# Three elementwise steps of an RWKV layer, from GpSimd to VectorE

## The chip, the cores and the metric

The kernel runs on one core of one Trainium2 chip. The metric is the device time of one execution in microseconds (us); the time of a kernel is the median of its runs.

## The reference, cut to what matters

A two-layer decoder over 1024 tokens of width 1024. The first layer is latent attention, the second an RWKV-7 mixer with 24 heads of width 64; each has four memory heads beside it, a SiLU gate and an output projection. All that the change touches is in the second layer:

```python
w = -jax.nn.softplus(-(w0 + jnp.tanh(wd) @ w2)) - 0.5
decay = jnp.exp(-jnp.exp(w))
a = jax.nn.sigmoid(a0 + ad @ a2)
kk = heads(k * k_k)
kk = kk / jnp.maximum(jnp.linalg.norm(kk, axis=-1, keepdims=True), 1e-12)
k = k * (1.0 + (a - 1.0) * k_a)
# one step of the scan
sa = jnp.einsum('bhvk,bhk->bhv', state, -kk_t)
state = state * w_t[:, :, None, :] + sa[..., None] * (kk_t * a_t)[:, :, None, :] + v_t[..., None] * k_t[:, :, None, :]
# after the scan
y = (y - mean) * lax.rsqrt(var + GN_EPS)
y = y * gn_w + gn_b
```

## The kernel before, in words

Activations lie with channels on the 128 partitions and 512 tokens along the free axis, so each of the two halves of the sequence is a tile of 128x512. A large matmul is done as three: every fp32 operand is split into a high part (rounded, fp32r) and a low part (the rest), and high by high, high by low and low by high are summed (mm3, L159 to L164). ScalarE (ACT) makes the high part of a weight tile (L153), and VectorE (DVE) or GpSimd (POOL) the low part (L155). In the RWKV layer VectorE makes all the low parts of the large weights.

The RWKV layer works through 24 items: 12 pairs of heads for the first half of the tokens, then the same 12 for the second half. An item passes five stages, and five items are under way at a time, one in each stage (layer1, the loop over `stages`):

- `project`: r, k and v by large matmuls;
- `prep`: the small decay weights w2 and a2 are loaded and split (L990 to L992) and multiplied (L996, L997); k is normed to kk (L1003 to L1016, with the reciprocal root of `rsqrt`, L194 to L199); then k is scaled (L1019), a is multiplied by kk (L1020), r*k is formed for the bonus (L1024), summed over a head by a matmul with a block of ones (L1042), and kk, r, a and k are scaled by the decay (L1049 to L1058);
- `invert`: 31 pairs of small VectorE instructions (L1139, L1143) solve triangular systems;
- `scan`: eight chunks one after the other, each a chain TensorE (L1215, L1217), VectorE (gm, L1219), TensorE (L1221), VectorE (SAV, L1222), TensorE (L1224), VectorE (the new state S, L1236);
- `norm`: squares, sum and `rsqrt` of the outputs (tile m), the scaling of the outputs by it (L1265), transposes on TensorE (L1269) and two VectorE steps (L1270, L1271).

The gate and output projections, large matmuls in groups of three (L162 to L164), are interleaved with these. A scheduler writes the final order of each engine's queue when the program is built, and each engine then works through its queue in that order; an instruction at the head of a queue that waits for another engine holds up all that stands behind it. The three tiles of the small weights (w2, w2h, w2l) have one buffer each, so the next item's split waits until this item's matmuls L996 and L997 have read them.

Of the kernel before, what the change touches and what calls it, by code (L numbers as in the profile page):

```python
# [13 lines left out]
F32 = mybir.dt.float32  # L14
# [4 lines left out]
ALU = mybir.AluOpType  # L19
# [52 lines left out]
class Build:  # L72
# [706 lines left out]
    def layer1(self, x1, first, second):  # L779

        nc, A, tc = self.nc, self.A, self.tc
        with ExitStack() as st:
# [158 lines left out]
            self.lows = True  # L941
            N, now = 2 * NH, [0]
            stages = [(project, ST[0]), (lambda i: self.prep(items[i], env), ST[1]), (lambda i: self.invert(items[i], env), ST[2]), (scan, ST[3]), (norm, ST[4])]
            extra = {}
            add = lambda step, gen, n: extra.setdefault(step, []).append((gen, n + 1))
# [33 lines left out]
    def prep(self, d, env):  # L979
# [6 lines left out]
        V, G, ACT = nc.vector, nc.gpsimd, nc.scalar  # L986
        ck = lambda t: t[:].rearrange("p (c t) -> p c t", t=64)

        w2, wh, wl = (self.w2p.tile([P, 256], dt, tag=s, name=self.name(s)) for s, dt in (("w2", F32), ("w2h", F32R), ("w2l", F32R)))
        nc.sync.dma_start(w2[:], self.A["w2a2"][p])  # L990
        ACT.copy(wh[:], w2[:])  # L991
        G.tensor_sub(wl[:], w2[:], wh[:].bitcast(F32))  # L992
        sig, a = self.g(s="sig"), self.g(s="a")
        for j, (t, bias) in enumerate(((sig, PW0), (a, PA0))):
            ps = a_tile()
# [19 lines left out]
        kk = sq  # L1015
# [1 line left out]
        rk = self.g(s="rk")  # L1017
        ACT.activation(rk[:], a[:], AF.Identity, bias=self.oka[:, p : p + 1], scale=self.pc(PKA + p))
        V.tensor_mul(k[:], rk[:], k[:])  # L1019
        G.tensor_mul(a[:], a[:], kk[:])  # L1020

        yield

# [59 lines left out]
        for i in range(4):  # L1083
            yield
            ps = a_tile()
            for j in range(2):
# [4 lines left out]
                out=AM[i][:], in0=ps[:].rearrange("p (c f) -> p c f", f=256),  # L1091
                in1=am.unsqueeze(1).broadcast_to([P, 2, 256]), op=ALU.mult,
# [158 lines left out]
    def norm(self, d, env):  # L1251

        p, bonus, Y, sg, y_tile = d["p"], d["bonus"], d["Y"], d["sg"], env["y_tile"]
        nc = self.nc
        V, G, ACT = nc.vector, nc.gpsimd, nc.scalar
        yg = Y[:].rearrange("p i (h v) -> p (i h) v", h=2)
        m = self.smp.tile([P, 24], F32, tag="m", bufs=2, name=self.name("m"))
        wide = lambda x: x.unsqueeze(2).broadcast_to([P, 8, 64])
        ys = self.g([P, 8, 64], s="ys")
        ACT.activation(ys[:], yg, AF.Square)  # L1260
        V.tensor_reduce(m[:, 8:16], ys[:], AX.X, ALU.add)
        V.tensor_scalar(m[:, 8:16], m[:, 8:16], 1.0 / 64, EPS_G, ALU.mult, ALU.add)
        self.rsqrt(m, 8)
        yield
        G.tensor_tensor(out=yg, in0=yg, in1=wide(m[:, 0:8]), op=ALU.mult)  # L1265
        yield
        ps = y_tile()
        for i in range(4):
            nc.tensor.transpose(ps[:, i * P : i * P + P], Y[:, i, :], self.ident)  # L1269
        V.scalar_tensor_tensor(bonus[:], ps[:], self.pc(PGW + p), bonus[:], ALU.mult, ALU.add)  # L1270
        V.scalar_tensor_tensor(sg[:], bonus[:], self.pc(PGB + p), sg[:], ALU.add, ALU.mult)  # L1271
# [107 lines left out]
```

## Time and profile before

| | before |
|---|---|
| median of 3 runs | 2585.66 us (2582.15 to 2588.03) |
| the profiled execution: its time, its span | 2576.96 us, 2575.1 us |
| granted TensorE clock over the span | 0.991 |
| the RWKV layer's items, from the first product a * kk to the end | about 1040 us to 2575 us |
| GpSimd: L1020, L1265, L992 | 24 instructions each |

A row of groups names the source line, engine, operation, output and inputs (buffer numbers left out), the shape and the count, then the time busy and the mean duration in ns, then the idle time of the engine just before, with what ended it. A row of the timeline begins with the start and the duration in us. A row of waits says which engine waited for what: us in total, how often, the longest. PE is TensorE's matmuls and PEld its weight loads; the ends of matmuls are modelled.

### The profile page before, as it was taken

The numbers are of one execution on the slowest core, as the hardware profiler recorded it, in microseconds if no ns is written. First come the engines' busy times: TensorE is split into PE (matmuls) and PEld (weight loads), VectorE is DVE, ScalarE is ACT, GpSimd is POOL, SyncE is SP. The second block draws the span as 40 slices with busy tenths as digits, with TensorE's granted clock in tenths as the row PEclk, the third lists the DMA queues.
The fourth block names the chain that finished last, engine by engine and source line by source line (L and its number), as shares of the span: only waits on it lengthen the run. The fifth ranks groups of instructions, "written<-read, shape, count | busy, mean of one in ns | idle before, by whom it ended". The sixth has DMA issues, their size and how long they took to land.

```text
span 2575.1 us, 39906 instructions
## 1 busy us (share of the span) xinstructions
PE 2440.8 (95%) x13298; PEld 2004.1 (78%) x13298; DVE 1897.9 (74%) x5492; ACT 1374.2 (53%) x2971; POOL 367.7 (14%) x416
## 2 busy tenths in 40 slices
PE   7899999999999999999999999999999999999997
PEld 5687778888888788877777777777777777778775
DVE  6755334777777646698888888788888888786975
ACT  5444335555545434565665666666665655654542
POOL 4332222222211330010000000000000010000000
PEclk9999999999999999999999999999999999999998
DMA  4252222111112444422122222322222222232341
GB/s 161 86 172 89 80 82 76 47 59 50 56 60 70 142 158 145 139 79 74 61 65 74 77 74 83 103 78 78 70 77 73 69 85 94 94 99 96 107 146 68
DMA packets 165983, 231.46 MB, mean 90 GB/s; under 512 B 46096, under 2 KB 67984, under 8 KB 165776
## 3 DMA queue, kind: packets, MB, share of 16 engines
q1 hardware_dynamic: 165776, 228.90, 27.1%
q8 instruction: 105, 1.72, 0.3%
q14 instruction: 102, 0.84, 0.1%
HBM read 187.66 MB, written 37.49 MB: 87 GB/s over the span
## 4 chain that ended last, share of the span: by engine, by line
PE 64%; DVE 19%; ACT 5%; issue 5%; DMA 2%; SPq 0%; POOL 0%; POOLq 0%; DVEq 0%; ACTq 0%
PE mm L162 12%; PE mm L164 12%; PE mm L163 12%; PE a L1088 3%; DVE U L1143 2%; DVE tmp L1139 2%; PE pt L726 2%; DVE wl L155 2%; PE po L162 1%; PE po L163 1%; PE c L1221 1%; PE po L164 1%; PE c L1224 1%; DVE u L1019 1%; PE c L1215 1%
## 5 line engine op out<-in xcount | busy, mean ns | idle before, releaser
L153 ACT CAST wh<-wr 128x512 fp32r<-128x512 f32 (+3 forms) x500 | 298.7, 600 | 442.8 <-PE mm L163 362.8
L162 PE MATMUL mm<-xnh,wh 128*128 128x512 f32 x912 | 376.5, 413 | 0.6 <-DVE qml L134 0.4
L164 PE MATMUL mm<-xnh,wl 128*128 128x512 f32 x912 | 370.7, 407 | 1.1 <-DVE wl L155 1.1
L163 PE MATMUL mm<-xnl,wh 128*128 128x512 f32 x912 | 370.0, 406 | 0.0
L155 DVE TENSOR_TENSOR wl<-wr,wh 128x512 fp32r<-128x512 f32 (+2 forms) x352 | 238.5, 679 | 115.8 <-ACT wh L153 84.2
L155 POOL TENSOR_TENSOR wl<-wr,wh 128x512 fp32r<-128x512 f32 (+1 forms) x148 | 186.5, 1264 | 575.9 <-ACT wh L153 445.0
L162 PE MATMUL mm<-yh,wh 128*128 128x512 f32 x492 | 199.7, 406 | 5.9 <-DVE xr L391 5.9
L164 PE MATMUL mm<-yh,wl 128*128 128x512 f32 x492 | 196.3, 399 | 0.2 <-DVE wl L155 0.2
L162 PEld LDWEIGHTS mm<-xnh,wh 128*128 128x128 f32 x912 | 172.7, 190 | 30.4 <-issue 3.3
L164 PEld LDWEIGHTS mm<-xnh,wl 128*128 128x128 f32 x912 | 172.6, 189 | 29.9 <-DVE wl L155 1.3
L163 PE MATMUL mm<-yl,wh 128*128 128x512 f32 x492 | 195.4, 397 | 0.0
L163 PEld LDWEIGHTS mm<-xnl,wh 128*128 128x128 f32 x912 | 173.0, 190 | 26.1 <-issue 0.8
L162 PE MATMUL mm<-xh,wh 128*128 128x512 f32 x416 | 168.1, 405 | 7.7 <-ACT xh L440 7.7
L1235 ACT ACTIVATE sc<-S,f 128x128 f32<-128x128 f32 x168 | 67.4, 401 | 195.3 <-DVE S L1236 184.0
L1143 DVE TENSOR_TENSOR U<-U,tmp 128x60 f32<-128x60 f32 (+24 forms) x744 | 159.7, 215 | 13.5
L163 PE MATMUL mm<-xl,wh 128*128 128x512 f32 x416 | 167.5, 403 | 2.0 <-DVE xl L441 2.0
L164 PE MATMUL mm<-xh,wl 128*128 128x512 f32 x416 | 167.1, 402 | 0.0
L1139 DVE TENSOR_TENSOR tmp<-As,U 128x60 f32<-128x60 f32 (+24 forms) x744 | 157.1, 211 | 13.3 <-DMA U<-in_cst_dram 0.2
L992 POOL TENSOR_TENSOR w2l<-w,w2h 128x256 fp32r<-128x256 f32 x24 | 20.8, 865 | 897.9 <-ACT w2h L991 859.4
L304 ACT ACTIVATE p<-b,sm 128x512 f32<-128x512 f32 (+2 forms) x144 | 83.0, 580 | 117.5 <-DVE sm L301 78.2
L391 DVE TENSOR_TENSOR xr<-mm,xr 128x512 f32<-128x512 f32 x123 | 84.4, 688 | 77.2 <-PE mm L164 76.8
L162 PEld LDWEIGHTS mm<-yh,wh 128*128 128x128 f32 x492 | 92.8, 189 | 24.3 <-DVE xr L391 3.8
(362 smaller groups left out, 6300.0 us busy)
## 6 DMA issues: line engine op xcount, KB each, us to landing
wr<-in_wu_dram SPq DMA_DIRECT2D x292, 256.0 KB, 2.6
wr<-in_wo_dram SPq DMA_DIRECT2D x122, 256.0 KB, 2.6
yr<-y SPq DMA_DIRECT2D x60, 256.0 KB, 3.7
As<-sysd SPq DMA_DIRECT2D x24, 512.0 KB, 4.3
y<-y SPq DMA_DIRECT2D x32, 256.0 KB, 2.0
y<-sg SPq DMA_DIRECT2D x32, 256.0 KB, 2.1
g<-u SPq DMA_DIRECT2D x24, 256.0 KB, 2.5
gt<-g SPq DMA_DIRECT2D x24, 256.0 KB, 2.8
```

Source lines behind the costliest of these rows:

```text
L153: nc.scalar.copy(hi[:, :n], raw[:, :n])
L155: sub(lo[:, :n], raw[:, :n], hi[:, :n].bitcast(F32))
L162: mm(ps, a[0], b[0], start=start, stop=False)
L163: mm(ps, a[0], b[1], start=False, stop=False)
L164: mm(ps, a[1], b[0], start=False, stop=stop)
L304: nc.scalar.activation(p[:, :own], ps[:, :own], AF.Exp, bias=sm[:, 0:1], accum_out=sm[:, 2 + i : 3 + i])
L391: nc.vector.tensor_add(xs[m][:], ps[:], xs[m][:])
L726: nc.tensor.transpose(pt[:, o : o + P], src, self.ident)
L1088: mm(ps[:, j * 256 : j * 256 + 256], BK[c // 4][:, c % 4, :], AR[:, c, :], start=True, stop=True)
L1139: E.tensor_tensor(out=tmp[:, 0:u, 0:n], in0=As[:, 0:u, u : u + 1].broadcast_to([P, u, n]), in1=U[:, u : u + 1, i0:8].broadcast_to([P, u, n ...
L1143: E.tensor_tensor(out=U[:, 0:u, i0:8], in0=U[:, 0:u, i0:8], in1=tmp[:, 0:u, 0:n], op=ALU.add)
L1235: ACT.activation(sc[:], cur, AF.Copy, scale=fc)
```

## The change

Three calls in `prep` and `norm` go from GpSimd to VectorE, operands and shapes as before: the low part of the small decay weights (w2l, 128x256), the product a * kk (128x512) and the scaling of the normed outputs (yT, 128x512). The memset of SAV (L1069) stays on GpSimd.

```diff
@@ prep
         ACT.copy(wh[:], w2[:])
-        G.tensor_sub(wl[:], w2[:], wh[:].bitcast(F32))
+        V.tensor_sub(wl[:], w2[:], wh[:].bitcast(F32))
@@ prep
         V.tensor_mul(k[:], rk[:], k[:])
-        G.tensor_mul(a[:], a[:], kk[:])
+        V.tensor_mul(a[:], a[:], kk[:])
@@ norm
         yield
-        G.tensor_tensor(out=yg, in0=yg, in1=wide(m[:, 0:8]), op=ALU.mult)
+        V.tensor_tensor(out=yg, in0=yg, in1=wide(m[:, 0:8]), op=ALU.mult)
```

The scheduler writes all queues anew from there on, so it is not only that 72 rows change engine. VectorE's queue in `prep` of the third item (k is u_2537, kk is sq_2580), before:

```order
L1016 SCALAR_TENSOR_TENSOR sq_2580_11877<-u_2537_11666,prm_102,a_2583_11898 128x512
L1143 TENSOR_TENSOR U_2570_11828<-U_2570_11828,tmp_2571_11829 128x20x3
L1019 TENSOR_TENSOR u_2537_11666<-rk_2584_11912,u_2537_11666 128x512
L1049 TENSOR_TENSOR sig_2565_11816<-sq_2580_11877,sig_2565_11816 128x512
L1024 SCALAR_TENSOR_TENSOR rk_2584_11912<-u_2520_11562,prm_102,u_2537_11666 128x512
L1057 TENSOR_TENSOR BK_2609_12011<-a_2566_11817,Dm_2593_11932 128x4x64
```

The same place after the change:

```order
L1016 SCALAR_TENSOR_TENSOR sq_2580_11877<-u_2537_11666,prm_102,a_2583_11898 128x512
L1139 TENSOR_TENSOR tmp_2571_11829<-As_2569_11826,U_2570_11828 128x19x4
L1019 TENSOR_TENSOR u_2537_11666<-rk_2584_11912,u_2537_11666 128x512
L1020 TENSOR_TENSOR a_2566_11817<-a_2566_11817,sq_2580_11877 128x512
L1024 SCALAR_TENSOR_TENSOR rk_2584_11912<-u_2520_11562,prm_102,u_2537_11666 128x512
L1049 TENSOR_TENSOR sig_2565_11816<-sq_2580_11877,sig_2565_11816 128x512
L1057 TENSOR_TENSOR BK_2609_12011<-a_2566_11817,Dm_2593_11932 128x4x64
```

The product a * kk (L1020) now stands ahead of L1024, whose result TensorE's L1042 reads, and L1049 has moved behind L1024. So it is with all 24 items: L1020 stands between L1019 and L1024; before, L1049 stood between them in 12 of the 24.

VectorE's queue in the scan of an item of the first half (S0_2828 is the state, gm_2916 the next chunk's first step), before:

```order
L1222 COPY SAV_2613_12040<-c_2901_13361 64x128
L1236 SCALAR_TENSOR_TENSOR S0_2828_13048<-c_2902_13364,f_2594_11936,sc_2903_13368 128x128
L155 TENSOR_TENSOR wl_2966_13665<-wr_2964_13663,wh_2965_13664 128x512
L1219 TENSOR_TENSOR gm_2916_13444<-c_2915_13441,cst_101 128x128
L829 SCALAR_TENSOR_TENSOR u_2911_13408<-mm_2910_13383,prm_102,u_2911_13408 128x511
```

The same place after the change:

```order
L829 SCALAR_TENSOR_TENSOR u_2911_13408<-mm_2910_13383,prm_102,u_2911_13408 128x511
L1139 TENSOR_TENSOR tmp_2812_12944<-As_2810_12941,U_2811_12943 128x24
L1222 COPY SAV_2613_12040<-c_2901_13361 64x128
L1143 TENSOR_TENSOR U_2811_12943<-U_2811_12943,tmp_2812_12944 128x24
L155 TENSOR_TENSOR wl_2966_13665<-wr_2964_13663,wh_2965_13664 128x512
L1139 TENSOR_TENSOR tmp_2812_12944<-As_2810_12941,U_2811_12943 128x16
L1236 SCALAR_TENSOR_TENSOR S0_2828_13048<-c_2902_13364,f_2594_11936,sc_2903_13368 128x128
L1143 TENSOR_TENSOR U_2811_12943<-U_2811_12943,tmp_2812_12944 128x16
L992 TENSOR_TENSOR w2l_3049_14067<-w2_3047_14065,w2h_3048_14066 128x256
L1139 TENSOR_TENSOR tmp_2812_12944<-As_2810_12941,U_2811_12943 128x8
L1143 TENSOR_TENSOR U_2811_12943<-U_2811_12943,tmp_2812_12944 128x8
L1219 TENSOR_TENSOR gm_2916_13444<-c_2915_13441,cst_101 128x128
```

The low part of the next item's small weights (L992) stands between one chunk's state (L1236) and the next chunk's gm (L1219), and waits there for ScalarE's w2h_3048.

VectorE's queue after the change at the last item's outputs (yT_5946), close to the end of the program:

```order
L198 SCALAR_TENSOR_TENSOR m_6058_27611<-m_6058_27611 128x8
L199 SCALAR_TENSOR_TENSOR m_6058_27611<-m_6058_27611 128x8
L1265 TENSOR_TENSOR yT_5946_27185<-yT_5946_27185,m_6058_27611 128x512
L155 TENSOR_TENSOR wl_6074_27669<-wr_6072_27667,wh_6073_27668 128x128
L155 TENSOR_TENSOR wl_6077_27678<-wr_6075_27676,wh_6076_27677 128x128
L1270 SCALAR_TENSOR_TENSOR rk_5666_25952<-y_6065_27641,prm_102,rk_5666_25952 128x512
```

Before, the same rows stood there without L1265, which was GpSimd's; the two low parts L155 now stand behind it.

## The prediction

> **What bounds the kernel now.** I read the page's busy times and chain first, then the stages of the RWKV layer, then the three GpSimd groups and what they overlap, then TensorE's waits. The page:
>
> ```profile
> PE 2440.8 (95%) x13298; PEld 2004.1 (78%) x13298; DVE 1897.9 (74%) x5492; ACT 1374.2 (53%) x2971; POOL 367.7 (14%) x416
> PE 64%; DVE 19%; ACT 5%; issue 5%; DMA 2%; SPq 0%; POOL 0%; POOLq 0%; DVEq 0%; ACTq 0%
> ```
>
> TensorE is busy 95% of the span, and the chain that ended last runs over it and, a fifth of the time, over VectorE; GpSimd's share of that chain is 0%. So a faster product or scaling on its own buys nothing. The RWKV layer in six stretches (columns: PE, PEld, DVE, ACT and POOL busy, each with its count):
>
> ```profile
> 1040.00:1250.00 210.00, 200.35 (x1047) 160.24 (x1046) 177.31 (x568) 129.15 (x269) 18.75 (x22) 1.00 0.26 85
> 1250.00:1500.00 250.00, 234.26 (x1331) 191.84 (x1330) 206.55 (x710) 145.03 (x326) 18.21 (x20) 1.00 0.24 76
> 1500.00:1750.00 250.00, 238.47 (x1297) 190.37 (x1295) 212.54 (x700) 161.58 (x349) 17.29 (x20) 1.00 0.25 81
> 1750.00:2000.00 250.00, 238.36 (x1351) 192.33 (x1351) 210.35 (x718) 157.79 (x353) 19.65 (x21) 1.00 0.24 78
> 2000.00:2250.00 250.00, 237.24 (x1307) 191.11 (x1308) 207.47 (x721) 149.55 (x325) 21.05 (x24) 0.99 0.26 84
> 2250.00:2575.00 325.00, 298.20 (x1581) 243.06 (x1579) 247.51 (x749) 146.33 (x323) 10.99 (x12) 0.98 0.30 102
> ```
>
> Over these 1535 us TensorE is busy 1446.9 and idle 88; VectorE is busy 1261.7 (82%) and idle 273. The matmuls stay as they are, so the most that the change could win is part of the 88 us, and it can lose where VectorE's fuller queue makes TensorE wait.
>
> **What VectorE gets.** The three groups that leave GpSimd:
>
> ```profile
> L1020 POOL TENSOR_TENSOR a<-a,sq 128x512 f32<-128x512 f32 x24 | 34.9, 1454 | 146.0 <-DVE sq L1016 134.5 <-DVE S L1236 6.3 <-DVE wl L155 5.1
> L1265 POOL TENSOR_TENSOR yT<-yT,m 128x512 f32<-128x512 f32 x24 | 28.7, 1196 | 407.8 <-DVE n L198 121.0 <-DVE m L199 111.3 <-DVE n L199 62.1
> L992 POOL TENSOR_TENSOR w2l<-w,w2h 128x256 fp32r<-128x256 f32 x24 | 20.8, 865 | 897.9 <-ACT w2h L991 859.4
> ```
>
> Their price on VectorE comes from neighbours of the same form, the first a plain product, the second a difference with a broadcast operand, the third the low part of a 128x256 tile:
>
> ```profile
> L1050 DVE TENSOR_TENSOR L<-u,L 128x512 f32<-128x512 f32 x24 | 16.3, 681 | 0.0
> L1029 DVE TENSOR_TENSOR Dm<-L 128x512 f32<-128x512 f32 x24 | 16.4, 682 | 0.0
> L129 DVE TENSOR_TENSOR mks<-mkr,mks 128x256 fp32r<-128x256 f32 x8 | 3.4, 422 | 0.6 <-ACT mks L128 0.3
> ```
>
> That is 24 x 0.681 + 24 x 0.682 + 24 x 0.422 = 16.3 + 16.4 + 10.1 = 42.8 us.
>
> **What VectorE loses.** The timeline shows VectorE standing still beside GpSimd's instructions. At the product:
>
> ```profile
> 1293.70 0.73 DVE L829 SCALAR_TENSOR_TENSOR u<-mm,prm,u 128x511 f32<-128x511 f32 x1
> 1294.21 1.29 POOL L1020 TENSOR_TENSOR a<-a,sq 128x512 f32<-128x512 f32 x1 [6.52 <-DVE sq L1016]
> 1294.36 1.69 DVE L1019 TENSOR_TENSOR u<-rk,u 128x512 f32<-128x512 f32 x1
> ...
> 1295.97 0.34 DVE L1236 SCALAR_TENSOR_TENSOR S<-c,f,sc 128x128 f32<-128x128 f32 x1
> ```
>
> L1019 has the form of L1050 but takes 1.69 us: it begins 0.15 us behind GpSimd's L1020 and ends 0.55 us after it, most of its own 0.68 us after GpSimd let go. And at the outputs:
>
> ```profile
> 1285.79 1.90 POOL L1265 TENSOR_TENSOR yT<-yT,m 128x512 f32<-128x512 f32 x1 [12.72 <-DVE n L197]
> ...
> 1286.77 0.94 DVE L198 SCALAR_TENSOR_TENSOR n<-n 128x8 f32<-128x8 f32 x1
> ```
>
> An instruction over 8 columns takes 0.94 us and ends with GpSimd's. The groups show that this is the rule:
>
> ```profile
> L1019 DVE TENSOR_TENSOR u<-rk,u 128x512 f32<-128x512 f32 x24 | 30.0, 1249 | 0.0
> L1049 DVE TENSOR_TENSOR sig<-sq,sig 128x512 f32<-128x512 f32 x24 | 19.6, 817 | 0.0
> L1024 DVE SCALAR_TENSOR_TENSOR rk<-u,prm,u 128x512 f32<-128x512 f32 x24 | 18.7, 781 | 0.0
> L1016 DVE SCALAR_TENSOR_TENSOR sq<-u,prm,a 128x512 f32<-128x512 f32 x24 | 17.8, 742 | 1.2 <-PE a L1013 1.1
> L198 DVE SCALAR_TENSOR_TENSOR n<-n 128x8 f32<-128x8 f32 x81 | 20.6, 255 | 0.1
> L198 DVE SCALAR_TENSOR_TENSOR m<-m 128x8 f32<-128x8 f32 x72 | 11.8, 163 | 0.2
> ```
>
> Against L1050, L1019 loses 30.0 - 16.3 = 13.7 us and L1049 3.3; against L1016, L1024 loses 0.9: 17.9 us, 51% of L1020's 34.9. The n rows of L198 lose 81 x (0.255 - 0.163) = 7.5 us, mostly beside L1265. So the floor of what VectorE gets back is 25.4 us, and the ceiling the three groups' whole 84.4 us. I take the 51% that L1020 shows for all three: 43 us. VectorE's net is then 0, between +17 and -42 us.
>
> The Trainium skill, "SBUF — State Buffer", section "Who interferes with whom", says why: a VectorE instruction with two inputs in SBUF and a GpSimd instruction that reads SBUF share a read port, and whichever starts second is blocked whole. By that rule the loss is the overlap and vanishes with the GpSimd instructions; the rows of L1019 agree (1249 ns against 681).
>
> **What lies on the path.** TensorE's longest waits in this layer, where the changed steps stand in front of it:
>
> ```profile
> PE a L1042 <- DVE rk L1024: 12.0, 15, 1.6
> PE c L1221 <- DVE gm L1219: 9.4, 17, 1.1
> PE a L1013 <- ACT sq L1010: 5.7, 7, 1.5
> PE c L1221 <- DVE m L198: 5.6, 4, 1.6
> ```
>
> *The product.* L1042 waits for L1024, which stands behind L1019. Before, the collisions put on that stretch, per item, 0.57 us (L1019) and (3.3 + 0.9) / 24 = 0.17 us (L1049, L1024), and in 12 of 24 items L1049 itself stands in it. After, L1020 stands in it always. Instructions of this size follow each other at 0.66 us (1293.70 to 1294.36 above). Per item: +0.66 - 0.57 - 0.17 - 0.66 x 12/24 = -0.41 us. Fifteen waits cut by 0.41 are 6.2 us; as some of the 15 are shorter than that, I take -5, between -10 (all but the shortest gone) and +2 (L1049, now late, is missed by ScalarE's copies behind it). What is late next is L1042's own place in TensorE's queue; the large matmuls ahead of it have room to move up.
>
> *The scaling of the outputs.* The neighbours of L1265 in VectorE's queue are the other rsqrt (n), whose end ScalarE's L1010 and then L1013 wait for, and gm. Before they lost up to 0.94 - 0.16 = 0.78 us per collision, after they stand behind 0.66. Of the 5.7 and 5.6 us above I take -1, between -11 and +3.
>
> *The small weights.* On GpSimd L992 waited 859 us for ScalarE in an otherwise empty queue, which cost nothing. On VectorE such a wait would hold the scan up. Here is one of seven places, of 24, where the new queue puts L992 (between S and gm) ahead of the moment at which w2h was ready before:
>
> ```profile
> 1267.78 0.35 DVE L1236 SCALAR_TENSOR_TENSOR S<-c,f,sc 128x128 f32<-128x128 f32 x1 [0.71 <-PE c L1224]
> ...
> 1269.04 0.29 DVE L1219 TENSOR_TENSOR gm<-c,cst 128x128 f32<-128x128 f32 x1
> ...
> 1271.81 0.41 ACT L991 CAST w2h<-w 128x256 fp32r<-128x256 f32 x1
> ...
> 1272.34 0.72 POOL L992 TENSOR_TENSOR w2l<-w,w2h 128x256 fp32r<-128x256 f32 x1 [25.66 <-ACT w2h L991]
> ```
>
> If nothing else moved, VectorE would stand from 1268.13 to 1272.22, 4.1 us. But TensorE's and ScalarE's queues are rewritten too: L996 and L997, which free the buffers, stand one chunk earlier in the new queue. I take 0; the other end is the rival below.
>
> *The end.* The last scaling, the only one for which TensorE visibly waits on GpSimd:
>
> ```profile
> 2537.91 0.17 DVE L199 SCALAR_TENSOR_TENSOR m<-m 128x8 f32<-128x8 f32 x1
> ...
> 2538.21 1.20 POOL L1265 TENSOR_TENSOR yT<-yT,m 128x512 f32<-128x512 f32 x1 [44.95 <-ACT wh L153]
> 2539.46 0.66 PE L1269 MATMUL y<-cst,yT 128*128 128x128 f32 x4 [1.56 <-POOL yT L1265]
> ```
>
> On VectorE it starts when L199 ends (2538.08) and ends 0.68 later at 2538.76 instead of 2539.41: -0.6 us. The two low parts behind it come 0.7 us later, under the same wait.
>
> **The sum.** -5 - 1 + 0 - 0.6 = -6.6 us. The profiled execution took 2576.96 us (span 2575.1), so 2570.4. It is 8.7 us below the median of the three runs, 2585.66, and 5.2 below the fastest of them; on the median the same difference gives **2579.1 us**, -0.26%.
>
> **The rivals.**
>
> *The waits go wholly.* TensorE's queue, if written as though VectorE were never held up, fits only after the change: then the 12.0 us of L1042 and the 5.6 of L1221 behind m vanish: 2585.66 - 12.0 - 5.6 - 0.6 = 2567.5. For it: these waits stand beside collisions. Against: TensorE also waits 9.4 us for gm, in 17 waits, and nothing in these rows ties those to GpSimd.
>
> *Nothing is left.* Queues that are written anew give back at other places what L1042 wins: of 88 us idle, 6.6 are soon dealt out again. 2585.7. For it: VectorE's net is 0, and the number of waits is large and each small.
>
> *VectorE stands at the head of its queue for w2h* (slower). Seven places at 4.1 us are 29 us in which gm, SAV and S cannot run. VectorE's idle time takes some back; with half of it reaching TensorE, 2579.1 + 14.5 = 2593.6. It decides from about 2 us at each of the seven (14 us, half of it 7, which eats the gain). For it: single buffers, and GpSimd's 859 us of waiting; against: L996 and L997 moved as well.
>
> *VectorE is the bound* (slower). If the long L1019 had another cause, VectorE would take on 42.8 us and give back none: its idle time falls from 273 to 230 us, by 16%; with TensorE's idle time growing alike, 88 x 0.16 = 14 us, and 0.33 us (0.66 less half of it) at 15 waits of L1042, 5 us: 2604.7. The timeline speaks against it. The Trainium skill, "Perfetto Trace Analysis", section "Optimizing Scalar/DVE Operations", says that work may be handed to GpSimd when VectorE is saturated, the opposite of this change, but adds that the shared port may void it; at 82% busy and with the collisions above, the trace sides with the second half.
>
> **How the numbers follow.** My forecast 0.42, the waits gone wholly 0.15, nothing left 0.20, the head of the queue 0.16, VectorE the bound 0.07. The rewritten order gives each a spread of some 5 us either way, an estimate (a twentieth of the 88). About 0.2%, 5.2 us, is what a measurement of this kernel can tell from no change, so the line lies at 2580.5: faster gets 0.27 of my forecast, the 0.15 and 0.03 of "nothing left", 0.45; within 0.2% gets 0.15 of the forecast, 0.14 of "nothing left" and 0.03 of the head of the queue, 0.32; slower the remaining 0.23. The range 2564 to 2598 holds the forecast, "wholly" less 3.5 us of its spread, and the head of the queue with 4.4 us of its; it leaves out VectorE as the bound and the tails.
>
> **What would show it.** Right: L1019, L1049 and L1050 all near 0.68 us; L198 (n) near 0.16; VectorE's busy time in the six stretches within 10 us of 1261.7; TensorE's wait on L1024 at 6 to 8 us instead of 12.0; L1269 at the end behind VectorE by about 0.6 us sooner. Wrong: L1019 still near 1.2 us; an idle time before VectorE's L992 of over 14 us put down to ScalarE's w2h; TensorE idle for 88 us or more in this layer.

## The result, and the profile after

| | before | after |
|---|---|---|
| median of 4 runs each, same chip | 2583.90 us (2580.30 to 2588.03) | 2543.18 us (2540.26 to 2545.34) |
| ratio, with its 95% interval | | 0.9833 (0.9810 to 0.9856) |
| the profiled execution: time, span | 2576.96 us, 2575.1 us | 2544.33 us, 2542.6 us |
| granted TensorE clock | 0.991 | 0.991 |

The change is faster by 40.7 us between the medians. The forecast was 6.6 us: the direction was right, the size six times too small, and the time lies below the range. The two profiled executions, both at a granted clock of 0.991, lie 32.6 us apart; before's is quicker than all four of its runs in the table.

Part of the 40.7 us goes with the granted clock, the share of its full speed that TensorE was granted over a run. The kernel before, timed again with each set of experiments, took 2584.22 to 2589.57 us in its runs at 0.987 and 2578.75 to 2580.78 us in those at 0.990. One straight line through the 88 runs whose clock is on record, with one slope for all kernels, gives 2.0 us for each 0.001 of clock. Brought to one clock by this line, the change is 36 us faster, an estimate that is good to about 2 us, as are all below that are said to be at one clock. Why the clock differs between kernels is not shown.

The page after, the rows for the engines and for the chain:

```profile
PE 2434.1 (96%) x13298; PEld 2003.9 (79%) x13298; DVE 1883.6 (74%) x5564; ACT 1371.9 (54%) x2971; POOL 285.0 (11%) x344
PE 69%; DVE 16%; ACT 6%; issue 3%; DMA 2%; SPq 0%; DVEq 0%; POOL 0%; ACTq 0%; POOLq 0%
```

VectorE has 72 instructions more and is busy 14 us less; its share of the chain falls from 19% to 16%, TensorE's rises from 64% to 69%. The RWKV layer in the same stretches as before (PE, PEld, DVE, ACT, POOL), and their sum:

```profile
1040.00:1250.00 210.00, 205.17 (x1076) 165.64 (x1074) 176.07 (x578) 133.34 (x279) 4.24 (x8) 1.00 0.28 91
1250.00:1500.00 250.00, 241.56 (x1372) 197.82 (x1371) 213.05 (x767) 148.80 (x341) 4.14 (x8) 1.00 0.25 79
1500.00:1750.00 250.00, 242.34 (x1334) 196.17 (x1333) 210.03 (x708) 160.57 (x339) 4.05 (x8) 1.00 0.26 84
1750.00:2000.00 250.00, 241.78 (x1369) 195.42 (x1368) 215.61 (x774) 167.33 (x373) 5.27 (x10) 1.00 0.24 76
2000.00:2250.00 250.00, 242.35 (x1367) 196.88 (x1365) 210.41 (x735) 148.37 (x332) 4.16 (x8) 1.00 0.29 91
2250.00:2543.00 293.00, 269.62 (x1417) 219.60 (x1416) 225.55 (x680) 132.00 (x287) 2.03 (x4) 0.97 0.31 104
sum 1503.00, PE 1442.82 PEld 1171.53 DVE 1250.72 ACT 890.41 POOL 23.90; mean PE 240.47 PEld 195.26 DVE 208.45 ACT 148.40 POOL 3.98
```

The layer is 32 us shorter (1535 to 1503), and 28 us of that is TensorE's idle time: 1535 - 1446.9 = 88 us before, 1503 - 1442.8 = 60 after. Every stretch has some of it: in each of the four middle ones TensorE is busy 241.6 to 242.4 of 250 us, where it was 234.3 to 238.5. VectorE's groups after:

```profile
L1265 DVE TENSOR_TENSOR yT<-yT,m 128x512 f32<-128x512 f32 x24 | 16.6, 690 | 0.1
L1020 DVE TENSOR_TENSOR a<-a,sq 128x512 f32<-128x512 f32 x24 | 16.5, 686 | 0.0
L1049 DVE TENSOR_TENSOR sig<-sq,sig 128x512 f32<-128x512 f32 x24 | 16.4, 684 | 0.0
L1019 DVE TENSOR_TENSOR u<-rk,u 128x512 f32<-128x512 f32 x24 | 16.4, 682 | 0.0
L198 DVE SCALAR_TENSOR_TENSOR n<-n 128x8 f32<-128x8 f32 x81 | 13.2, 163 | 0.1
L992 DVE TENSOR_TENSOR w2l<-w,w2h 128x256 fp32r<-128x256 f32 x23 | 9.7, 420 | 1.0 <-ACT w2h L991 1.0
```

The moved instructions cost what their neighbours cost (690, 686, 420 ns). L1019 is down from 1249 to 682 ns, L198 (n) from 255 to 163. L992 waits for w2h 1.0 us in all. TensorE's waits in the layer:

```profile
PE y L1269 <- ACT yT L1244: 4.8, 19, 0.6
...
PE a L1042 <- DVE rk L1024: 3.3, 4, 1.4
PE c L1221 <- DVE gm L1219: 3.1, 8, 1.0
PE c L1221 <- DVE m L195: 1.8, 2, 1.0
PE a L1013 <- ACT sq L1010: 0.8, 4, 0.3
```

L1042 waits 3.3 us instead of 12.0, L1221 behind gm 3.1 instead of 9.4 and behind m 1.8 instead of 5.6, L1013 0.8 instead of 5.7. Together these four rows fell by 23.7 us, most of the 28; some smaller waits grew. And the end of the program in the timeline:

```profile
2505.85 0.17 DVE L199 SCALAR_TENSOR_TENSOR m<-m 128x8 f32<-128x8 f32 x1
2506.05 0.69 DVE L1265 TENSOR_TENSOR yT<-yT,m 128x512 f32<-128x512 f32 x1
...
2506.89 0.63 PE L1269 MATMUL y<-cst,yT 128*128 128x128 f32 x4 [0.72 <-DVE yT L1265]
```

From L199's end to L1269's start it is 2506.89 - 2506.02 = 0.87 us, before 2539.46 - 2538.08 = 1.38.

### The profile page after: what moved, and what is told of

It is laid out like the page before. It is cut to its first block, busy times and chain, and to the rows that moved or that the text cites. A ratio compares the mean times of both kernels' runs of the same rounds, so it can differ in the third digit from the quotient of the medians.

```text
span 2542.6 us, 39928 instructions
## 1 busy us (share of the span) xinstructions
PE 2434.1 (96%) x13298; PEld 2003.9 (79%) x13298; DVE 1883.6 (74%) x5564; ACT 1371.9 (54%) x2971; POOL 285.0 (11%) x344
## 4 chain that ended last, share of the span: by engine, by line
PE 69%; DVE 16%; ACT 6%; issue 3%; DMA 2%; SPq 0%; DVEq 0%; POOL 0%; ACTq 0%; POOLq 0%
PE mm L162 14%; PE mm L163 13%; PE mm L164 13%; PE a L1088 3%; DVE tmp L1139 2%; PE c L1221 2%; PE pt L726 2%; DVE U L1143 2%; PE c L1224 1%; PE po L162 1%; PE y L1228 1%; PE po L163 1%; DVE wl L155 1%; PE y L1227 1%; PE po L164 1%
## 5 line engine op out<-in xcount | busy, mean ns | idle before, releaser
L155 DVE TENSOR_TENSOR wl<-wr,wh 128x512 fp32r<-128x512 f32 (+2 forms) x352 | 237.2, 676 | 98.7 <-ACT wh L153 79.8
L155 POOL TENSOR_TENSOR wl<-wr,wh 128x512 fp32r<-128x512 f32 (+1 forms) x148 | 186.3, 1263 | 579.4 <-ACT wh L153 446.0
L1069 POOL MEMSET SAV<- 64x512 f32 x48 | 24.9, 524 | 1385.6 <-DVE m L1261 250.7
```

The source lines that it names most:

```text
L155: sub(lo[:, :n], raw[:, :n], hi[:, :n].bitcast(F32))
```

## The experiments

"Standstill" below is counted in each trace instruction by instruction: what a VectorE instruction that overlaps a GpSimd one takes beyond the lower quartile of its own line and shape. Before, this gives 21.2 us beside L1020, 13.9 beside L1265 and 8.4 beside L992, 43.5 in all; after, 0. (VectorE's busy time in the layer, with the same queue, falls by 39.5 us from before to x_free, 1261.7 to 1222.2, so the count is good to some 10%.) Theory: these standstills cost time almost one to one, because the queues were written as if they did not exist. First rival: the time comes from the rewritten queues, whatever VectorE gets back. Second rival: it is a matter of how much work VectorE has. A third, the prediction's own, is the place of the product ahead of L1024. A fourth is the granted clock, which was 0.985 to 0.988 in the runs of e2_norm and 0.991 to 0.993 in those of i_rope; the last column takes it out by the line of 2.0 us for each 0.001.

| run | what it is | median, us | ratio (95%) | less than before, us | the same at one clock (estimate) |
|---|---|---|---|---|---|
| x_free | before's queues, GpSimd reads next to nothing | 2543.74 | 0.9844 (0.9827 to 0.9861) | 41.5 | 40 |
| x_collide | the change's queues, 72 spare readers on GpSimd | 2573.81 | 0.9956 (0.9939 to 0.9972) | 11.4 | 9 |
| x_known | the change, the same 72 on VectorE | 2560.99 | 0.9915 (0.9893 to 0.9936) | 24.7 | 23 |
| f_prod | before's queues, no product on GpSimd | 2569.95 | 0.9942 (0.9925 to 0.9959) | 15.8 | 14 |
| f_norm | before's queues, no scaling on GpSimd | 2572.43 | 0.9950 (0.9931 to 0.9970) | 13.3 | 13 |
| e1_prod | only the product moved | 2566.10 | 0.9935 (0.9919 to 0.9952) | 19.1 | 18 |
| e2_norm | only the scaling moved | 2582.80 | 0.9994 (0.9985 to 1.0003) | 2.4 | 5 |
| e12_prodnorm | these two moved | 2552.33 | 0.9876 (0.9860 to 0.9892) | 33.4 | 29 |
| e3_w2l | only the small weights moved | 2575.05 | 0.9969 (0.9955 to 0.9982) | 9.2 | 6 |
| i_swap | the change, product ahead of the scaling of k | 2552.30 | 0.9876 (0.9860 to 0.9892) | 32.0 | 31 |
| i_late | the change, product behind the bonus | 2548.98 | 0.9866 (0.9845 to 0.9886) | 35.3 | 33 |
| i_rope | the change, and three steps of the first layer | 2535.72 | 0.9813 (0.9796 to 0.9829) | 48.6 | 41 |

The column before the last is taken between medians that were timed together; before's lay between 2584.3 and 2585.72 us.

### Standstill or queues: x_free and x_collide

x_free keeps the queues of TensorE, VectorE and ScalarE exactly as before. What GpSimd read becomes a memset, which reads nothing, but for 8 of the product's 512 columns; the kernel leaves this work out:

```diff
-        G.tensor_sub(wl[:], w2[:], wh[:].bitcast(F32))
+        G.memset(wl[:].bitcast(F32), 0.0)
...
-        G.tensor_mul(a[:], a[:], kk[:])
+        G.tensor_mul(a[:, 0:8], a[:, 0:8], kk[:, 0:8]); G.memset(a[:, 8:T], 0.5)
...
-        G.tensor_tensor(out=yg, in0=yg, in1=wide(m[:, 0:8]), op=ALU.mult)
+        G.memset(Y[:], 0.0)
```

> The kernel before with every queue of TensorE, VectorE and ScalarE in the order of before, but GpSimd no longer reads in the three places: the low part of the small weights and the scaling of the outputs are GpSimd memsets (0), and of the product a * kk only 8 of 512 columns are formed, the others set to 0.5 (this work is left out). Theory C (collisions: the gain of 41 us came from VectorE no longer standing still beside GpSimd): nothing is added to VectorE and the standstills go, so at least the gain of the change, 2530 to 2550 us, with L1019 near 0.68 us and TensorE's idle time in the RWKV layer some 25 to 45 us lower. Theory Q (queues: the gain came from the scheduler's new order, the collisions cost little): 2572 to 2584 us.

It took 2543.74 us, as fast as the change (2543.18) by the medians and some 4 us faster at one clock, with not one row of these three queues moved. The layer as one stretch, then two of VectorE's groups and one of GpSimd's:

```profile
1040.00:2542.00 1502.00, 1443.45 (x7910) 1173.42 (x7909) 1222.16 (x4164) 889.18 (x1943) 63.17 (x143) 0.99 0.28 87
```

```profile
L1019 DVE TENSOR_TENSOR u<-rk,u 128x512 f32<-128x512 f32 x24 | 16.4, 682 | 0.0
L198 DVE SCALAR_TENSOR_TENSOR n<-n 128x8 f32<-128x8 f32 x81 | 13.0, 160 | 0.1
L1265 POOL MEMSET yT<- 128x512 f32 x24 | 12.8, 532 | 321.3 <-ACT ys L1260 232.8 <-PE mm L164 60.0 <-DVE tmp L1139 25.1
```

TensorE is idle 1502 - 1443.45 = 58.6 us, as after the change. GpSimd still works beside VectorE (63 us), but these memsets hold nothing up, and the standstill beside them is under 1 us. TensorE's waits for gm, which the prediction tied to nothing on GpSimd, fall with it, and so do those of L1042 and L1013; L1221's behind m stay:

```profile
PE c L1221 <- DVE m L198: 5.2, 5, 1.2
...
PE c L1221 <- DVE gm L1219: 3.7, 8, 1.0
...
PE a L1042 <- DVE rk L1024: 1.5, 4, 0.5
...
PE a L1013 <- ACT sq L1010: 0.8, 3, 0.3
```

So the rewriting of the queues is not needed for the gain. The memsets are also shorter than what they replace (532 ns against 1196), and they need not wait for m or kk. But before, the only wait for GpSimd that TensorE, VectorE or ScalarE shows in this layer is TensorE's for the last L1265 (1.56 us, at the end that the prediction shows), and that is the most that x_free can have won by this.

x_collide goes the other way: the changed kernel's queues exactly, and 72 further GpSimd instructions that read, one for each moved one (that for the product stands later in `prep`, behind L1050), in place in tiles that nothing reads any more:

```diff
         V.tensor_sub(wl[:], w2[:], wh[:].bitcast(F32))
+        G.tensor_sub(w2[:], w2[:], wh[:].bitcast(F32))
...
         V.tensor_mul(L[:], r[:], L[:])
+        G.tensor_mul(r[:], r[:], r[:])
...
+        G.tensor_tensor(out=ys[:], in0=ys[:], in1=wide(m[:, 0:8]), op=ALU.mult)
         V.tensor_tensor(out=yg, in0=yg, in1=wide(m[:, 0:8]), op=ALU.mult)
```

> The changed kernel with every queue of TensorE, VectorE and ScalarE in its order, but 72 GpSimd instructions without a reader put back, of the old shapes, each in place in a tile that is dead by then: the difference on w2 behind L992, the scaling of ys by m ahead of L1265, and a product on r behind L1050 (the old one ran beside L1019, an instruction or two earlier). Theory C: VectorE stands still beside them as before and does the moved work besides, 2570 to 2600 us. Theory Q: the order is unchanged, so 2541 to 2552 us.

It took 2573.81 us: about 30 us of the 40.7 are gone again (27 of the 36 at one clock). The layer, two groups of VectorE and one of GpSimd:

```profile
1040.00:2572.00 1532.00, 1452.31 (x7926) 1172.54 (x7924) 1282.85 (x4237) 891.98 (x1946) 115.83 (x119) 0.99 0.28 86
```

```profile
L1265 DVE TENSOR_TENSOR yT<-yT,m 128x512 f32<-128x512 f32 x24 | 24.7, 1028 | 0.1
L198 DVE SCALAR_TENSOR_TENSOR n<-n 128x8 f32<-128x8 f32 x81 | 16.8, 208 | 0.1
L1050 POOL TENSOR_TENSOR u<-u 128x512 f32<-128x512 f32 x24 | 44.5, 1855 | 197.4 <-DVE rk L1024 121.3 <-DVE L L1050 68.1 <-PE mm L162 8.1
```

VectorE does the same 4237 instructions as after the change and shows 1282.85 us instead of 1250.72: the count by instruction gives 33.9 us of standstill (18.2 beside the spare L1265, 8.1 and 7.5 beside the others). TensorE is idle 1532 - 1452.3 = 80 us instead of 60. In the timeline one can watch it pass on:

```profile
1291.67 1.05 POOL L1265 TENSOR_TENSOR ys<-ys,m 128x512 f32<-128x512 f32 x1 [18.59 <-DVE n L198]
1291.73 1.54 DVE L1265 TENSOR_TENSOR yT<-yT,m 128x512 f32<-128x512 f32 x1
...
1293.33 0.28 DVE L1219 TENSOR_TENSOR gm<-c,cst 128x128 f32<-128x128 f32 x1
...
1293.66 0.49 PE L1221 MATMUL c<-gm,XT 128*128 128x128 f32 x2 [0.43 <-DVE gm L1219]
```

VectorE's L1265 begins 0.06 us behind GpSimd's, takes 1.54 us instead of 0.69, and gm is the next but one in its queue; TensorE's L1221 waits for it. That is a wait of the kind that the prediction left untouched, and in this run it is back at most of its size:

```profile
PE c L1221 <- DVE gm L1219: 7.6, 14, 1.2
PE a L1013 <- ACT sq L1010: 5.7, 11, 1.0
```

Per us of standstill: 41.5 / 43.5 = 0.95 in x_free, about 30 / 33.9 = 0.9 in x_collide; at one clock 40 / 43.5 = 0.9 and 27 / 33.9 = 0.8. That the spare readers also let their tiles go later is not excluded in x_collide; x_free, which has no spare readers, gives a price near to it.

### The same work where the queues know of it: x_known

As x_collide, with the 72 spare instructions on VectorE (V for G in its three added lines).

> The changed kernel with the same 72 spare instructions as in the run with collisions put back, but on VectorE instead of GpSimd: 43 us more work for VectorE in the RWKV layer, which the scheduler sees when it writes the queues. If VectorE's work is absorbed as long as the queues are written for it, and only the standstill that no queue was written for costs time: 2541 to 2552 us. If VectorE's time counts whatever it is made of: 2570 to 2590 us.

It took 2560.99 us: 16 to 18 us for 42.5 us of additional VectorE work (13 at one clock), neither of the two expectations. The layer and two of the groups:

```profile
1040.00:2558.00 1518.00, 1452.94 (x7920) 1173.47 (x7919) 1285.23 (x4308) 889.38 (x1945) 23.89 (x46) 0.99 0.28 87
```

```profile
L1050 DVE TENSOR_TENSOR u<-u 128x512 f32<-128x512 f32 x24 | 16.4, 681 | 0.0
L1265 DVE TENSOR_TENSOR ys<-ys,m 128x512 f32<-128x512 f32 x24 | 16.4, 685 | 0.1
```

VectorE shows as much busy time as in x_collide (1285.2 and 1282.9), and TensorE is idle 65 us instead of 80. So the same busy time on VectorE costs about 0.4 us per us where it stands in the queues (0.3 at one clock), and 0.9 (0.8) where it is standstill. This is one order of the queues, and a tenth or two of the 0.4 can be that order's (the runs on the order alone, below). Of the 15 us by which the layer is longer than after the change, only 5 are idle time of TensorE; the other 10 are its busy time, 1452.9 us against 1442.8 for nearly as many instructions (7920 and 7926), part of it by the clock (0.988 against 0.991), the rest unexplained. Work is not free on VectorE. The change's own 42.8 us cost little: x_free, which does without them, is as fast by the medians and 4 us faster at one clock.

### One part at a time

With before's queues kept, f_prod and f_norm each apply one line of x_free's diff, the second and the last.

> The kernel before, all queues of TensorE, VectorE and ScalarE in its order, but of the product a * kk GpSimd forms only 8 of 512 columns and sets the others to 0.5 (this work is left out). One for one: 21 us less, 2562 to 2567 us. If the path to L1042 alone counted, as the prediction had it: its 12 us of waits, 2573 to 2579 us.

> The kernel before, all queues of TensorE, VectorE and ScalarE in its order, but the scaling of the outputs is a GpSimd memset to 0 that reads nothing (this work is left out). If every microsecond that VectorE stands still beside GpSimd is a microsecond of time, as the two runs with all three groups say (41 us for 43, 31 us for 34), 14 us less: 2569 to 2574 us. If the scaling's collisions fall where nothing waits, and moving it gained nothing for that reason: 2580 to 2586 us.

They won 15.8 us (standstill beside L1020: 21.2) and 13.3 us (beside L1265: 13.9), 0.75 and 0.96 per us. By the 95% intervals these are 0.5 to 0.9 and 0.6 to 1.3, so they can't be told apart. f_norm lies in its first range; f_prod lies between its two, 3 us above one for one. In f_norm the product's collisions stay and only the others go; in f_prod it is the reverse. f_norm, then f_prod:

```profile
L1019 DVE TENSOR_TENSOR u<-rk,u 128x512 f32<-128x512 f32 x24 | 30.8, 1284 | 0.0
L198 DVE SCALAR_TENSOR_TENSOR n<-n 128x8 f32<-128x8 f32 x81 | 13.9, 171 | 0.1
```

```profile
L1019 DVE TENSOR_TENSOR u<-rk,u 128x512 f32<-128x512 f32 x24 | 16.4, 682 | 0.0
L198 DVE SCALAR_TENSOR_TENSOR n<-n 128x8 f32<-128x8 f32 x81 | 19.5, 241 | 0.1
```

The next four make one or two of the change's three edits, and the queues are rewritten each time.

> Only the product a * kk goes to VectorE. Theory C: of 43 us that VectorE stood still beside the three groups, counted instruction by instruction in the trace of before, 21 us were beside the product, so about half of the gain, 2560 to 2568 us. Theory Q: a third order, no relation to the share: the three single parts do not add up to 41 us.

> Only the scaling of the outputs goes to VectorE. Theory C: 14 of the 43 us, so about a third of the gain, 2567 to 2575 us. Theory Q: as for the product alone, no relation to the share.

> The product and the scaling go to VectorE, the small weights stay on GpSimd. One for one: 35 of the 43 us of standstill go, 2548 to 2553 us. If the scaling gains nothing whatever stands beside it: as with the product alone, 2563 to 2568 us.

> Only the low part of the small weights goes to VectorE. One for one with its standstill: 8 us less, 2574 to 2580 us. If it only helps beside the other two: 2581 to 2587 us. If VectorE stands at the head of its queue for w2h (the prediction's rival): 2588 us or more.

They won 19.1, 2.4, 33.4 and 9.2 us, the first, third and fourth as one for one had it. The second missed: by the medians, moving the scaling alone gave nothing that can be told from no change, although VectorE got the standstill beside L1265 back. Part of this is the clock, the lowest of all kernels in its ten runs: at one clock it won 5 us, still short of the 14. Its queues had a longer wait elsewhere:

```profile
PE a L1042 <- DVE rk L1024: 15.7, 17, 2.5
```

That is 3.7 us more than before, and together with the product the scaling is worth 33.4 - 19.1 = 14.3 us, about what f_norm gives. The other parts roughly add: 19.1 + 14.3 + 9.2 = 42.6 against 40.7, and at one clock 18 + 11 + 6 = 35 against 36. That the rest of e2_norm's miss is the luck of its order is likely but not shown; why this order would be a poor one was not found.

### The order alone: i_swap and i_late

Both are the changed kernel with the same work, the product in another place of `prep`.

```diff
+        V.tensor_mul(a[:], a[:], kk[:])
         V.tensor_mul(k[:], rk[:], k[:])
-        V.tensor_mul(a[:], a[:], kk[:])
```

> The changed kernel with the product a * kk written ahead of the scaling of k instead of behind it: the same work, no GpSimd reader, and queues that the scheduler writes anew. It measures what a rewriting alone moves: 2538 to 2550 us if the spread is small; 10 us or more away from 2543 would say that a difference of 10 us between two of these kernels can be the order alone.

i_late takes it out from between L1019 and L1024, where the prediction had it cost L1042 0.66 us per item:

```diff
         V.tensor_mul(k[:], rk[:], k[:])
-        V.tensor_mul(a[:], a[:], kk[:])
...
+        V.tensor_mul(a[:], a[:], kk[:])
         V.tensor_mul(Dx[:], kk[:], Dx[:])
```

> The changed kernel with the product a * kk written behind the bonus, just ahead of the scaling by the decay, so that it no longer stands between L1019 and L1024. The prediction's term for the path to L1042: 0.66 us less at each of the four waits that are left, 3 us or less: 2538 to 2543 us, and TensorE's wait for L1024 near zero.

They took 2552.30 and 2548.98 us, 9 and 5 to 6 us more than the change (i_late's interval overlaps the change's, i_swap's does not). At one clock it is 5 and 2 us, and the second can't be told from nothing. i_swap lies 2 us above its range, and i_late was expected to win. The wait that it was to cut (L1042 is line 1041 in it, L1024 line 1023) was already small and stayed:

```profile
PE a L1041 <- DVE rk L1023: 3.1, 3, 1.4
```

3.1 us against 3.3: the place of the product ahead of L1024 cost nothing. In these two cases rewriting the queues by itself moved the median by up to 9 us, 2 to 5 us at one clock.

### Further in the same direction: i_rope

In the changed kernel, three steps of the first layer whose GpSimd instructions read two tiles go to VectorE as well; by the count they held VectorE up by 7.7, 4.7 and 4.5 us.

```diff
-                nc.gpsimd.tensor_mul(sw[:], sw[:], sin[:, sl])
+                nc.vector.tensor_mul(sw[:], sw[:], sin[:, sl])
...
-                    nc.gpsimd.tensor_sub(a[64:128, :], t[0:64, :], a[0:64, :].bitcast(F32))
-                    nc.gpsimd.tensor_sub(b[0:64, :], t[64:128, :], b[64:128, :].bitcast(F32))
+                    nc.vector.tensor_sub(a[64:128, :], t[0:64, :], a[0:64, :].bitcast(F32))
+                    nc.vector.tensor_sub(b[0:64, :], t[64:128, :], b[64:128, :].bitcast(F32))
```

> The changed kernel with the three GpSimd readers of the attention layer's rotations (L523, L640, L641: 38 instructions) on VectorE too; VectorE stood still beside them for some 17 us. One for one: 2524 to 2530 us. If standstill costs only where TensorE waits for VectorE (in the attention stretch from 300 to 1040 us TensorE is idle for 16 us of 740): 2539 to 2545 us.

It took 2535.72 us (2535.47 to 2536.14), the fastest kernel of the study: below all runs of the change (2540.26 and up), though those were timed at another time and the intervals of the two ratios overlap. It lies between its two expectations. 7.5 us for 16.9 us of standstill is 0.44 per us; at one clock it is 5 us, 0.3 per us. In this part of the program TensorE has less to win. The stretch of 300 to 700 us, after the change and in i_rope:

```profile
300.00:700.00 400.00, 394.11 (x2243) 331.47 (x2242) 242.91 (x557) 193.48 (x448) 93.10 (x126) 1.00 0.20 63
```

```profile
300.00:700.00 400.00, 395.49 (x2280) 335.14 (x2278) 251.15 (x586) 198.08 (x456) 60.33 (x103) 1.00 0.20 63
```

TensorE is idle 5.9 us of 400 in the first and 4.5 in the second. That is 1.4 us of the gain; where the rest comes from was not followed.

## Why the prediction was right in direction and wrong in size

**What VectorE gets and loses: right.** 42.8 us of work was the price, and the three rows after give 16.6 + 16.5 + 9.7 = 42.8. 43 us of standstill was estimated from the 51% of L1020; the count gives 43.5. The busy time in the layer fell from 1261.7 to 1250.7 us, 11 where "within 10" was written, and L1019, L1049 and L198 came to the durations named.

**"VectorE's net is then 0": the step that failed.** The busy time does not change by much, and the prediction took that to mean that only a few local waits could: its sum holds 6.6 us, and TensorE's idle time in the layer alone fell by 28. But the 43 us that go and the 42.8 us that come are not of one kind. The one was in no queue's reckoning: every standstill pushed back what stood behind it in a fixed order, and cost 0.75 to 0.96 us of time per us (x_free, f_norm, f_prod, x_collide; 0.7 to 1.0 at one clock). The other stands in queues that were written with it; the next 42.5 us of that kind cost about 0.4 per us (x_known). By x_free's price the standstill alone is 43.5 x 0.95 = 41 us, and measured were 40.7, so that by the medians the moved work cost nothing; at one clock it is 40 against 36, so that it cost some 4 us, 0.1 per us. At x_known's price it would have cost 42.8 x 0.4 = 17 us and the change would have won only 24; why the change's own work was so much cheaper than the next 42.5 us is not shown. VectorE's 18% of idle time did not absorb the standstill. That it lies at other moments than the collisions is argued, not shown.

**The product, -5: mechanism not confirmed.** The wait of L1042 for L1024 fell by 8.7 us, not 5. The working had L1049 and L1020 change places ahead of L1024; i_late shows that the place made no difference (3.1 against 3.3 us), and in x_free that wait falls to 1.5 us with the queue unmoved. What held it was the standstill of L1019 and of the rows ahead of it.

**The scaling, -1: mis-sized.** The waits that it was taken from, L1013's and L1221's behind m, fell by 4.9 and 3.8 us. That is near the end of -11 that was kept for the range, not the -1 chosen from the 0.66 us that stands in the collision's place. Only the first is the standstill's: L1013's wait falls to 0.8 us in x_free too, while L1221's behind m stays there at 5.2 of 5.6 us, so its fall in the change came with the rewritten queues. L1221's wait for gm, which no term held, fell by 6.3; x_free, with 3.7 us of 9.4, shows that most of it was standstill.

**The small weights, +0, and the end, -0.6: right in what they priced.** L992 waited 1.0 us for w2h, not 29. What the first term left out is the standstill beside L992 (8.4 us): its move alone won 9.2 us, 6 at one clock. The end came 0.5 us sooner.

**The rivals.** "The waits go wholly" named the mechanism that x_free shows, queues written as though VectorE were never held up; its 2567.5 us was still 24 us too high, since it let go only the waits of L1042 and L1221 behind m, of which x_free shows the second to stay. "Nothing is left" is refuted by TensorE's 60 idle us; the head of the queue by L992's row; VectorE as the bound by L1019's 682 ns and 1250.7 us.

**What stays open.** Whether the moved work is nearly free or costs more that a lucky order gives back: x_free and the change lie within 0.6 us of each other by the medians and 4 us apart at one clock, and an order alone can be worth 5 to 9. Why the scaling moved alone gives so little. And why the granted clock of one kernel's runs differs from another's.

## What to carry to other kernels

When an instruction of one engine takes longer than its twins beside another engine's, count that excess by itself and price it at 0.7 to 1 us of time per us where TensorE waits on that engine as here, apart from work that the queues know of; a net of busy times hides it. To learn what such a standstill costs before moving work, keep all queues and replace the reading instruction by one that only writes. Before medians a few us apart are compared, look at the granted clock of each run: 0.001 was worth 2 us here. A single order of the queues is worth several us either way here, so a gain of that size in one rewritten kernel shows nothing about its cause.

## What the runs showed of the hardware that was not expected

A GpSimd memset of 128x512 (532 ns) holds up no VectorE instruction with two inputs: with 24 of them in place of the scaling, L198 (n) took 160 ns in x_free. The Trainium skill, "SBUF — State Buffer", section "Who interferes with whom", says that a VectorE instruction with two inputs contends with a GpSimd instruction that reads SBUF, not with one that only writes; x_free agrees.

An instruction with one input is another matter. In the change, the memset of SAV holds up L1262, which takes 0.56 us here and 162 ns in the median, and ends 0.03 us after the memset:

```profile
2083.54 0.56 DVE L1262 TENSOR_SCALAR m<-m 128x8 f32<-128x8 f32 x1
2083.55 0.52 POOL L1069 MEMSET SAV<- 64x512 f32 x1 [71.51 <-DVE m L1261]
```

So a memset is not a harmless stand-in beside every VectorE instruction.

GpSimd is held up in its turn: of the 24 spare products on r in x_collide the shortest took 1041 ns, the median 2093 and the longest 2560. Ahead of the five of 2092 to 2096 ns, VectorE's L1049 (128x512, two inputs) had begun some 0.16 us earlier.

The time stood still counts as VectorE's busy time in the profile. In x_collide that engine looks 32 us busier than after the change with the same 4237 instructions, so a busy share does not tell work from waiting.
